# Program order on every engine, with empty work pieces, in a streaming encoder layer (RG-LRU and gMLP branches)

## The chip, the cores and the metric

One Trainium2 chip; the program runs on one of its cores. The metric is the device time of one execution in microseconds (us). A change is told from no change if it is over about 0.2%, some 5 us.

## The reference

One layer on 256 positions (tokens) with 4096 channels, everything in float32:

```python
hn = rmsnorm(x, norm_g)
xa, ga, u, v, gb = split(hn @ w_in, [4096, 8192, 12288, 16384])       # w_in: 4096 x 20480
xa = causal_depthwise_conv(xa, conv_w, conv_b)                        # 4 taps
ya = rg_lru(xa, w_a, b_a, w_x, b_x, lam)                              # 16 heads of 256 channels
vn = layernorm(gelu(v))                                               # over 4096 channels
yb = gelu(u) * (W_s @ vn + b)                                         # 16 groups, 128 x 128 over positions
x = x + concat([ya * silu(ga), yb * silu(gb)]) @ w_out                # 8192 x 4096
out = rmsnorm(x, final_g)
```

In `rg_lru`, r and i are sigmoids of block-diagonal products of xa, `log a = -8 r softplus(-lam)`, and `h_t = a_t h_{t-1} + sqrt(1 - a_t^2) (i x)_t` is a scan over the positions.

## The kernel before, in words

Every product is made in float32 precision from three matmuls: an operand is split into `hi` (a copy in the reduced type float32r, on ScalarE, L63) and `lo` (the rest, on VectorE, L64), and hi·hi, hi·lo and lo·hi are added up in PSUM. The weights, 480 MB, are read once, in chunks of 128 x 1024 floats (512 KB). A chunk is loaded into `raw` by a DMA that SyncE issues (L100; 4 buffers), split into `hi` and `lo` (4 buffers each), and used by 12 matmuls of 512 columns. `take` (L136) hands out the next chunk and, before that, starts the loads and splits that keep three chunks ahead (`AHEAD`). The sequence of all chunks is the list `plan`.

The stages, e counting 0 to 7:

- Branch A, for each e: `project_t(X_A + e)`, 16 chunks that give 512 columns of xa; `project_t(G_A + e)`, 16 chunks for 512 columns of ga (the "gate slab" below), with two hooks, behind its chunks 10 and 14, that make the gate products of the two heads of e (`pgate`, 24 matmuls of 256 columns each, from a chunk of `w_g`); and `out_project` of e − 1, 16 chunks of `w_out`. For e = 0 the hooks are in the X slab of e = 1 (chunks 6 and 10).
- `project_t(V_T + n)`, n = 0 to 7, with `out_project` of branch A's e = 7 behind the first.
- Branch B, for each e: `project_t(U_T + e)`, `project_t(G_T + e)`, the mixing over positions (`mix_tokens`, `pm`), and `out_project` of e − 1 (from e = 1 on).
- The last half slab of `w_out`: chunks ("o", 30, n), and the 8 chunks ("o", 31, n), split beforehand into tiles that stay (`resident`), so that the rows of the first 128 positions are finished first.

All else that a slab needs is put into the list `todo` as small pieces. `work(n)` (L144) runs n of them, fractions adding up; it is called behind each chunk's matmuls. `flush` runs all that are left, `reach(m)` runs up to piece m. The front of an X slab (`queue_front`) is: two evictions from PSUM (ACT), two transpositions of 32 x 32 blocks (`turn`, DVE, L276, into `tr`), four `move` pieces of four DMAs each on SyncE (L281), which put the blocks into place, then `settle` (ACT copy), the four-tap convolution `conv` (four DVE instructions a piece) and the split of its result into `yh` and `yl`, which the gate products read. The side of a gate slab (`queue_side`) is: two silu pieces, two turns, four moves into `ga`; then `queue_scans` with reciprocals (L425), POOL products, scans, and the split into `mix`, which `out_project` of the next e reads. Branch B's `queue_mix` turns and moves `u` (through `gb`) and splits it in four `halve` pieces.

So the program text lists, chunk by chunk: load and split of chunk c + 3, matmuls of chunk c, some pieces. The kernel before gives that text to a scheduler, which sets each engine's order by its own estimate of when things are ready; on an engine the instructions then run in the order that it set. The names and lines that the change touches are `queue_front` (L350), `load_spatial` (L527), `queue_normalise` (L536), `queue_mix` (L581), `resident` (L596), the loop of branch B from L599 and the last loops.

Of the kernel before, what the change touches and what calls it, by code (L numbers as in the profile page):

```python
# [7 lines left out]
F32 = mybir.dt.float32  # L8
F32R = mybir.dt.float32r
# [4 lines left out]
P = 128  # L14
# [9 lines left out]

@with_exitstack
def hybrid_trunk(ctx: ExitStack, tc: tile.TileContext, x, xt, par, w_t, w_g, ln_g, ln_b, ws_t, w_o, f_g, out):

# [2 lines left out]
    nc = tc.nc  # L32
# [111 lines left out]
    def work(n):  # L144

        credit[0] += n
        while credit[0] >= 1 and todo:
            todo.pop(0)()
            done[0] += 1
            credit[0] -= 1  # L150
        credit[0] %= 1

    def flush():
        work(len(todo))
# [196 lines left out]
    def queue_front(e, ps):  # L351

        t = a1.tile([P, 2, 512], F32, tag="t", name="t")
        xc = a1.tile([P, 4, S], F32, tag="c", name="xc")

        def evict(m):
            nc.scalar.activation(t[:, m, :], ps[:, m, :], AF.Copy, scale=rstd_tok[:, m : m + 1])

        todo.append(lambda: evict(0))
        todo.append(lambda: evict(1))  # L360
        tr = a1.tile([P, 1024], F32, name="tr")
        flat = t.rearrange("p m x -> p (m x)")
        queue_turned(flat, t, tr)

        def settle(i):
            own = xc[:, 2 * i : 2 * i + 2, :].rearrange("p c (m a t) -> p (c m) a t", m=2, a=4)
            nc.scalar.copy(own, in_order(flat, 4 * i, 4))

        todo.append(lambda: None)
        todo.append(lambda: settle(0))  # L370
        y = queue_x(2 * e, xc[:, 0:2, :])
        halves.append(queue_split(y))
        todo.append(lambda: settle(1))
        return [y, queue_x(2 * e + 1, xc[:, 2:4, :])]
# [145 lines left out]
    for n in range(1, 8):  # L520
        queue_v(n, project_t(V_T + n))
    todo.append(v_stats)
    flush()

    def load_spatial(e):  # L527
        raw = b1.tile([P, 2, P], F32, name="ws")
        hi = b1.tile([P, 2, P], F32R, name="ws_hi")
        lo = b1.tile([P, 2, P], F32R, name="ws_lo")  # L530
        nc.sync.dma_start(raw, ws_t[2 * e : 2 * e + 2].rearrange("g j i -> j g i"))
        nc.gpsimd.memset(raw[64:128, :, 0:64], 0.0)  # L532
        split(hi, lo, raw)
        return hi, lo

    def queue_normalise(h):  # L536
        cs = slice(h * S, (h + 1) * S)
        vh = b1.tile([P, 2, S], F32R, name="vh")
        vl = b1.tile([P, 2, S], F32R, name="vl")

        def one():
            affine = b1.tile([P, 2, S], F32, tag="tmp", name="affine")
            gain, shift = affine[:, 0, :], affine[:, 1, :]
            nc.sync.dma_start(gain, ln_g[:, cs].partition_broadcast(P))
            nc.sync.dma_start(shift, ln_b[:, cs].partition_broadcast(P))
            for m in range(2):
                nc.vector.tensor_scalar(  # L547
                    v[:, m, cs], v[:, m, cs], mv[:, m, 0:1], rv[:, m : m + 1], op0=ALU.subtract, op1=ALU.mult
                )
                nc.gpsimd.tensor_tensor(v[:, m, cs], v[:, m, cs], gain, op=ALU.mult)  # L550
                nc.gpsimd.tensor_tensor(v[:, m, cs], v[:, m, cs], shift, op=ALU.add)

        todo.append(one)
        todo.append(lambda: split(vh, vl, v[:, :, cs]))
        return vh, vl

# [24 lines left out]
    def queue_mix(u, gb, mix):  # L581

        flat = u.rearrange("p m x -> p (m x)")
        queue_turned(flat, u, gb.rearrange("p m x -> p (m x)"))

        def halve(c):
            hi, lo = (mix[:, c, h, :].rearrange("p (m a t) -> p m a t", m=2, a=4) for h in range(2))
            split(hi, lo, in_order(flat, 2 * c, 2))

        todo.append(lambda: None)  # L590
        for c in range(4):
            todo.append(lambda c=c: halve(c))

    res = []

    def resident(n):  # L596
        res.append(load_split(("o", 31, n), resp, resp, f"r{n}"))

    pending = None  # L599
    vn = queue_normalise(0)  # L600
    flush()
    for e in range(8):
        ws = load_spatial(e)
        ps = project_t(U_T + e)
        flush()
        u = b1.tile([P, 2, 512], F32, name="u")
        queue_u(u, ps)
        flush()
        pms = [mix_tokens(0, ws, vn)]
        queue_gating(2 * e, pms[0], u)  # L610
        vn = queue_normalise(2 * e + 1)
        gb = b1.tile([P, 2, 512], F32, name="gb")
        queue_silu(gb, project_t(G_T + e), b1, "tmp")
        pms.append(mix_tokens(1, ws, vn))
        queue_gating(2 * e + 1, pms[1], u)
        todo.append(lambda u=u, gb=gb: nc.gpsimd.tensor_tensor(u, u, gb, op=ALU.mult))  # L616
        if e < 7:
            vn = queue_normalise(2 * e + 2)
            if pending is not None:
                out_project(*pending, items=2)  # L620
            mix = mixp.tile([P, 4, 2, S], F32R, tag="mix", name="mix")
            queue_mix(u, gb, mix)
            pending = (8 + e, mix)
# [2 lines left out]
    resp = ctx.enter_context(tc.tile_pool(name="resp", bufs=1, side="right"))  # L626
    fin = ctx.enter_context(tc.tile_pool(name="fin", bufs=1))
    fin2 = ctx.enter_context(tc.tile_pool(name="fin2", bufs=2))
    fg = fin.tile([P, D], F32, name="fg")
    ssq = fin.tile([P, 2, 9], F32, name="ssq")  # L630
    mix = fin.tile([P, 4, 2, S], F32R, name="mix")
    nc.sync.dma_start(fg, f_g.partition_broadcast(P))
    queue_mix(u, gb, mix)
    out_project(*pending, extra=lambda n: resident(n - 3) if n >= 3 else None)
    flush()


    for n in range(8):
        ps = [po.tile([P, 512], F32, tag="po", name="po_t") for _ in range(2)]
        chunk = take("o", 30, n)  # L640
        for m in range(2):
            for j in range(2):
                out_step(ps[m], mix, j, chunk, j, m, j == 0, j == 1)
        for m in range(2):
            add_out(ps[m], m, n)
        if n in (0, 2, 4):
            resident(5 + n // 2)
    part = fin.tile([P, 1], F32, name="part")
    for m in range(2):
        for n in range(8):  # L650
            ns = slice(n * 512, (n + 1) * 512)

            parts = 2 if (m, n) == (1, 7) else 1
            for h in range(parts):
                w = 512 // parts
                hs = slice(n * 512 + h * w, n * 512 + (h + 1) * w)
                ps = po.tile([P, 512], F32, tag="po", name="po_t")
                for j in range(2):
                    hi, lo = (t[:, :, h * w : (h + 1) * w] for t in res[n])
                    out_step(ps[:, :w], mix, 2 + j, (hi, lo), j, m, j == 0, j == 1)  # L660
                nc.vector.tensor_tensor(acc[:, m, hs], ps[:, :w], acc[:, m, hs], op=ALU.add)
                t = fin2.tile([P, 512], F32, name="sqt")
                nc.scalar.activation(t[:, :w], acc[:, m, hs], AF.Square, accum_out=ssq[:, m, n + h : n + h + 1])
            if m == 0 or n < 6:
                nc.gpsimd.tensor_tensor(acc[:, m, ns], acc[:, m, ns], fg[:, ns], op=ALU.mult)
            if (m, n) == (1, 6):
                nc.vector.tensor_reduce(part, ssq[:, 1, 0:7], axis=mybir.AxisListType.X, op=ALU.add)
            work(1)
        tot = fin2.tile([P, 1], F32, name="tot")
        rs = fin2.tile([P, 1], F32, name="rs")  # L670
        if m == 0:
            nc.vector.tensor_reduce(tot, ssq[:, 0, 0:8], axis=mybir.AxisListType.X, op=ALU.add)
        else:
            nc.vector.scalar_tensor_tensor(tot, ssq[:, 1, 7:8], part, ssq[:, 1, 8:9], op0=ALU.add, op1=ALU.add)
        rsqrt_mean(rs, tot, fin2, D, f"out{m}")

        def finish(m, n, rs):
            ns = slice(n * 512, (n + 1) * 512)
            if m and n >= 6:
                nc.vector.scalar_tensor_tensor(acc[:, m, ns], acc[:, m, ns], rs, fg[:, ns], op0=ALU.mult, op1=ALU.mult)  # L680
            elif n % 2:
                nc.vector.tensor_scalar(acc[:, m, ns], acc[:, m, ns], rs, None, op0=ALU.mult)
            else:
                nc.scalar.mul(acc[:, m, ns], acc[:, m, ns], rs)
            nc.sync.dma_start(out_v[:, m, ns], acc[:, m, ns])

        for n in range(8):
            todo.append(lambda m=m, n=n, rs=rs: finish(m, n, rs))
# [39 lines left out]
```

## Time and profile before

| | us |
|---|---|
| median of 3 runs | 2522.48 (2522.43 to 2522.57) |
| the profiled execution's own time | 2522.99 |
| its span, first to last instruction | 2521.2 |
| TensorE (PE) busy | 2503.9, 99% |
| VectorE (DVE) busy | 1598.9, 63% |
| ScalarE (ACT) busy | 1216.4, 48% |
| GpSimd (POOL) busy | 221.6, 9% |
| HBM read | 494.03 MB, 198 GB/s over the span |

The granted TensorE clock is at 0.998 of full speed over the span. A matmul of 512 columns shows 389 ns, but starts 0.227 us behind the one before: they overlap. SyncE issues nearly all DMAs and has no busy time in the profile; what it issues and waits for is in the timeline and in the list of waits. "Idle before" in a row is the engine's idle time before that instruction, and the name behind it ended the wait.

### The profile page before, as it was taken

How to read it: one execution, taken by the hardware profiler on the slowest of the kernel's cores; microseconds unless marked ns; L12 is line 12 of the kernel's file. 1: busy time of each engine (PE TensorE's matmuls, PEld its weight loads, DVE VectorE, ACT ScalarE, POOL GpSimd, SP SyncE). 2: the span in 40 equal slices, each digit the busy share in tenths (PEclk: the TensorE clock that was granted, in tenths of full speed). 3: DMA queues.
4: the chain of work that ended last, by engine and by line, in shares of the span. 5: the costliest groups of instructions: out<-in, count | busy, mean ns of one | idle time of the engine just before them, and what ended most of it. 6: DMA issues, size and time to landing. Idle time of an engine off the chain costs nothing.

```text
span 2521.2 us, 30308 instructions
## 1 busy us (share of the span) xinstructions
PE 2503.9 (99%) x11214; PEld 2078.5 (82%) x11214; DVE 1598.9 (63%) x1735; ACT 1216.4 (48%) x1393; POOL 221.6 (9%) x164
## 2 busy tenths in 40 slices
PE   9999999999999999999999999999999999999997
PEld 8888888888888888888888888888888888888886
DVE  6687584858576676855444475565647474746477
ACT  7665454646464545544444444444444444444444
POOL 0021020201011110200000011010101010101002
PEclk9999999999999999999999999999999999999999
DMA  9666666566656566666656666665656566666674
GB/s 341 218 201 198 199 200 198 188 202 194 219 194 207 193 210 199 212 196 192 193 193 194 195 195 208 198 206 193 209 192 211 192 210 192 209 191 206 225 218 148
DMA packets 166276, 512.83 MB, mean 203 GB/s; under 512 B 22256, under 2 KB 44912, under 8 KB 166000
## 3 DMA queue, kind: packets, MB, share of 16 engines
q1 hardware_dynamic: 165984, 510.88, 62.9%
q8 instruction: 88, 1.44, 0.2%
q14 instruction: 60, 0.49, 0.1%
q10 hardware_dynamic: 144, 0.02, 0.0%
HBM read 494.03 MB, written 4.19 MB: 198 GB/s over the span
## 4 chain that ended last, share of the span: by engine, by line
PE 90%; DVE 4%; SPq 1%; DMA 1%; issue 1%; ACT 1%; POOL 1%; DVEq 0%; POOLq 0%; ACTq 0%
PE ps L257 22%; PE ps L256 22%; PE ps L258 22%; PE po_t L307 7%; PE po_t L308 7%; PE po_t L306 7%; DVE lo L64 2%; SPq L281 1%; DMA raw<-in_w_out 1%; PE pgate L394 0%; PE pgate L393 0%; PE pgate L392 0%; DMA raw<-in_w_t 0%; ACT hi L63 0%; DVE acc L312 0%
## 5 line engine op out<-in xcount | busy, mean ns | idle before, releaser
L64 DVE TENSOR_TENSOR lo<-raw,hi 128x1024 fp32r<-128x1024 f32 (+1 forms) x914 | 1134.7, 1245 | 835.5 <-ACT hi L63 826.8
L63 ACT CAST hi<-raw 128x1024 fp32r<-128x1024 f32 (+1 forms) x914 | 958.3, 1051 | 1164.2 <-PE ps L258 833.1
L257 PE MATMUL ps<-lo,xs 128*128 128x512 f32 x2560 | 996.4, 389 | 0.8 <-DVE lo L64 0.8
L256 PE MATMUL ps<-hi,xs 128*128 128x512 f32 x2560 | 996.7, 389 | 0.0
L258 PE MATMUL ps<-hi,xs 128*128 128x512 f32 x2560 | 996.0, 389 | 0.0
L258 PEld LDWEIGHTS ps<-hi,xs 128*128 128x128 f32 x2560 | 480.6, 188 | 100.2
L257 PEld LDWEIGHTS ps<-lo,xs 128*128 128x128 f32 x2560 | 480.7, 188 | 100.0 <-DVE lo L64 1.1
L256 PEld LDWEIGHTS ps<-hi,xs 128*128 128x128 f32 x2560 | 480.7, 188 | 99.7 <-ACT hi L63 0.5
L307 PE MATMUL po_t<-lo,mix 128*128 128x512 f32 x1026 | 399.6, 389 | 1.7 <-DVE lo L64 1.7
L306 PE MATMUL po_t<-hi,mix 128*128 128x512 f32 x1026 | 399.4, 389 | 0.6 <-DVE acc L312 0.3
L308 PE MATMUL po_t<-hi,mix 128*128 128x512 f32 x1026 | 399.2, 389 | 0.0
L307 PEld LDWEIGHTS po_t<-lo,mix 128*128 128x128 f32 x1026 | 192.6, 188 | 43.0 <-DVE lo L64 2.8
L306 PEld LDWEIGHTS po_t<-hi,mix 128*128 128x128 f32 x1026 | 192.6, 188 | 41.8 <-ACT hi L63 1.4
L308 PEld LDWEIGHTS po_t<-hi,mix 128*128 128x128 f32 x1026 | 192.6, 188 | 40.2
L312 DVE TENSOR_TENSOR acc<-po_t,acc 128x512 f32<-128x512 f32 x256 | 165.1, 678 | 1.6 <-PE po_t L308 1.6
L413 POOL TENSOR_TENSOR gate_i<-gate_i,y 128x512 f32<-128x512 f32 x16 | 26.9, 1679 | 707.1 <-ACT gate_i L405 614.0
L550 POOL TENSOR_TENSOR v<-v,affine 128x256 f32<-128x256 f32 x32 | 31.3, 996 | 526.3 <-DVE v L547 387.0
L425 DVE RECIPROCAL gate_r<-gate_r 128x256 f32<-128x256 f32 x32 | 55.5, 1734 | 0.0
L532 POOL MEMSET ws<- 64x128 f32 x8 | 1.6, 200 | 562.8 <-DMA ws<-in_ws_t 488.5
L429 POOL TENSOR_TENSOR gate_i<-gate_i,gate_r 128x512 f32<-128x512 f32 x16 | 32.6, 2037 | 176.3 <-DVE gate_r L425 176.3
L337 DVE SCALAR_TENSOR_TENSOR y<-xc,prm,y 128x254 f32<-128x254 f32 (+2 forms) x96 | 42.5, 476 | 0.3
L616 POOL TENSOR_TENSOR u<-u,gb 128x1024 f32<-128x1024 f32 x8 | 20.0, 2495 | 204.1 <-DVE gb L298 202.9
(111 smaller groups left out, 868.8 us busy)
## 6 DMA issues: line engine op xcount, KB each, us to landing
raw<-in_w_t SPq DMA_DIRECT2D x638, 512.0 KB, 4.3
raw<-in_w_out SPq DMA_DIRECT2D x256, 512.0 KB, 4.2
raw<-in_w_g SPq DMA_DIRECT2D x16, 512.0 KB, 4.4
acc<-in_x SPq DMA_DIRECT2D x8, 512.0 KB, 9.2
t<-tr SPq DMA_DIRECT2D x128, 32.0 KB, 2.1
ga<-tr SPq DMA_DIRECT2D x128, 32.0 KB, 1.9
u<-gb SPq DMA_DIRECT2D x128, 32.0 KB, 4.0
out<-acc SPq DMA_DIRECT2D x16, 256.0 KB, 2.6
```

Source lines behind the costliest of these rows:

```text
L63: nc.scalar.copy(hi, src)
L64: sub.tensor_tensor(lo, src, hi.bitcast(F32), op=ALU.subtract)
L256: nc.tensor.matmul(ps[:, m, :], lhsT=xs[:, k, 0, ms], rhs=hi[:, j, :], start=k == 0, stop=False)
L257: nc.tensor.matmul(ps[:, m, :], lhsT=xs[:, k, 0, ms], rhs=lo[:, j, :], start=False, stop=False)
L258: nc.tensor.matmul(ps[:, m, :], lhsT=xs[:, k, 1, ms], rhs=hi[:, j, :], start=False, stop=k == KT - 1)
L306: nc.tensor.matmul(ps, lhsT=mix[:, k, 0, ms], rhs=hi[:, j, :], start=start, stop=False)
L307: nc.tensor.matmul(ps, lhsT=mix[:, k, 0, ms], rhs=lo[:, j, :], start=False, stop=False)
L308: nc.tensor.matmul(ps, lhsT=mix[:, k, 1, ms], rhs=hi[:, j, :], start=False, stop=stop)
L312: nc.vector.tensor_tensor(acc[:, m, ns], ps, acc[:, m, ns], op=ALU.add)
L337: nc.vector.scalar_tensor_tensor(y[:, c, back:], xk[:, : S - back], prm_col(C_W + 3 - back, k), y[:, c, back:], op0=ALU.mult, op1=ALU.add)
L425: nc.vector.reciprocal(r[:, c, :], r[:, c, :])
L429: nc.gpsimd.tensor_tensor(gi, gi, r, op=ALU.mult)
```

## The change

The program is built with `manual_schedule`: every engine issues its instructions in the order of the program text. In the text itself:

- empty pieces (`pause`) are put between a piece and the one that reads its result: two before `settle` and before `halve` (one each before), three in the normalisation of v, two before the split of `ws`, which becomes a piece;
- three `flush` calls of branch B go, its `out_project` runs one piece per chunk instead of two, and the last one 1.25;
- the resident chunks get raw buffers of their own (`rraw`, 2), and each is split one call after its load;
- `final_g` is loaded in four parts, near the end, instead of in one before the last `out_project`.

```diff
+    def pause(n):
+        for _ in range(n):
+            todo.append(lambda: None)
...
@@ queue_front
-        todo.append(lambda: None)
+        pause(2)
         todo.append(lambda: settle(0))
...
     todo.append(v_stats)
-    flush()
...
@@ load_spatial
-        split(hi, lo, raw)
+        pause(2)
+        todo.append(lambda: split(hi, lo, raw))
...
@@ queue_normalise
         todo.append(one)
+        pause(3)
         todo.append(lambda: split(vh, vl, v[:, :, cs]))
...
@@ queue_mix
-        todo.append(lambda: None)
+        pause(2)
         for c in range(4):
             todo.append(lambda c=c: halve(c))
...
     def resident(n):
-        res.append(load_split(("o", 31, n), resp, resp, f"r{n}"))
+
+        if n < 8:
+            raw = rraw.tile([P, 2, 512], F32, name="rraw")
+            nc.sync.dma_start(raw, w_o[31, n])
+            res.append((resp.tile([P, 2, 512], F32R, name=f"r{n}hi"), resp.tile([P, 2, 512], F32R, name=f"r{n}lo"), raw))
+        if n:
+            split(*res[n - 1])
...
     vn = queue_normalise(0)
-    flush()
     for e in range(8):
         ws = load_spatial(e)
         ps = project_t(U_T + e)
         flush()
         u = b1.tile([P, 2, 512], F32, name="u")
         queue_u(u, ps)
-        flush()
...
             if pending is not None:
-                out_project(*pending, items=2)
+                out_project(*pending)
...
+    rraw = ctx.enter_context(tc.tile_pool(name="rraw", bufs=2))
...
-    nc.sync.dma_start(fg, f_g.partition_broadcast(P))
     queue_mix(u, gb, mix)
-    out_project(*pending, extra=lambda n: resident(n - 3) if n >= 3 else None)
+    out_project(*pending, extra=lambda n: resident(n - 3) if n >= 3 else None, items=1.25)
...
-        if n in (0, 2, 4):
+        if n in (0, 2, 4, 6):
             resident(5 + n // 2)
+        if n >= 4:
+            ns = slice((n - 4) * 1024, (n - 3) * 1024)
+            nc.sync.dma_start(fg[:, ns], f_g[:, ns].partition_broadcast(P))
...
-    with tile.TileContext(nc) as tc:
+    with tile.TileContext(nc) as tc, tc.manual_schedule():
         hybrid_trunk(tc, *args)
```

The change shifts line numbers, by 1 up to `work` and by 5 behind it: L100 before is L101 after it, L281 is L286. Two places show what it does to the order.

SyncE, from the loads of an X slab of branch A (e = 2 or later) on, before; `t<-tr` are the moves of the front (four to a piece), `raw<-in_w_t` the loads of the slabs, `raw<-in_w_g` those of the gate products:

```order
L100 DMA raw<-in_w_t 128x1024 x24
L281 DMA t<-tr 32x256 x12
L100 DMA raw<-in_w_t 128x1024
L281 DMA t<-tr 32x256 x4
L100 DMA raw<-in_w_t 128x1024 x2
L100 DMA raw<-in_w_g 128x1024
```

and with the change:

```order
L101 DMA raw<-in_w_t 128x1024 x23
L286 DMA t<-tr 32x256 x8
L101 DMA raw<-in_w_t 128x1024
L286 DMA t<-tr 32x256 x4
L101 DMA raw<-in_w_t 128x1024
L286 DMA t<-tr 32x256 x4
L101 DMA raw<-in_w_t 128x1024 x2
L101 DMA raw<-in_w_g 128x1024
```

The loads of gate chunks 7 to 9 now alternate with the moves; before, 24 loads (up to gate chunk 7) came ahead of all moves. In the same way the side's moves, one block of 16 behind 12 loads of `w_out` before, now stand in fours behind loads 8 to 11.

DVE in the gate slab of e = 1, before; `tr<-t` are the turns, `y<-xc` the convolution, `yl` what the gate products read:

```order
L276 STREAM_TRANSPOSE tr<-t 128x4x4x32 x2
L64 TENSOR_TENSOR lo<-raw,hi 128x1024
L64 TENSOR_TENSOR mix<-sq_1255,mix 128x2x256
L64 TENSOR_TENSOR lo<-raw,hi 128x1024 x6
L335 TENSOR_SCALAR y<-xc,prm 128x256 x2
L337 SCALAR_TENSOR_TENSOR y<-xc,prm,y 128x255 x2
```

and with the change:

```order
L65 TENSOR_TENSOR mix<-sq_1252,mix 128x2x256
L65 TENSOR_TENSOR lo<-raw,hi 128x1024
L281 STREAM_TRANSPOSE tr<-t 128x4x4x32
L65 TENSOR_TENSOR lo<-raw,hi 128x1024
L281 STREAM_TRANSPOSE tr<-t 128x4x4x32
L65 TENSOR_TENSOR lo<-raw,hi 128x1024 x3
L340 TENSOR_SCALAR y<-xc,prm 128x256
```

The turns moved behind the last split into `mix`, and three chunks' `lo` instead of seven now lie between the second turn and the convolution.

## Rows read from the trace of the kernel before

**Rows 1.** The page, part 1: busy us, share of the span, instructions

```profile
PE 2503.9 (99%) x11214; PEld 2078.5 (82%) x11214; DVE 1598.9 (63%) x1735; ACT 1216.4 (48%) x1393; POOL 221.6 (9%) x164
```

**Rows 2.** Waits of TensorE: line, releaser: us in total, times, longest us

```profile
PE po_t L307 <- DVE lo L64: 1.7, 3, 1.0
...
PE ps L257 <- DVE lo L64: 0.8, 1, 0.8
PE po_t L306 <- DVE acc L312: 0.3, 1, 0.3
PE po_t L306 <- ACT hi L63: 0.3, 1, 0.3
```

**Rows 3.** Timeline, steady stretch in the gate slab of e = 4: start, length

```profile
565.02 0.39 PE L256 MATMUL ps<-hi,xs 128*128 128x512 f32 x1
...
567.74 0.39 PE L256 MATMUL ps<-hi,xs 128*128 128x512 f32 x1
...
566.30 1.22 DVE L64 TENSOR_TENSOR lo<-raw,hi 128x1024 fp32r<-128x1024 f32 x1 [1.50 <-ACT hi L63]
```

**Rows 4.** Waits of SyncE's queue, whole span

```profile
SPq L100 <- DVE lo L64: 1699.3, 780, 5.3
```

**Rows 5.** Timeline, front of e = 4 in its gate slab, DVE and SyncE

```profile
559.29 1.30 DVE L276 STREAM_TRANSPOSE tr<-t 128x512 f32<-128x512 f32 x2
...
573.18 1.23 DVE L64 TENSOR_TENSOR lo<-raw,hi 128x1024 fp32r<-128x1024 f32 x1 [2.93 <-ACT hi L63]
...
574.98 1.66 DVE L337 SCALAR_TENSOR_TENSOR y<-xc,prm,y 128x255 f32<-128x255 f32 x4
...
568.51 0.33 SPq L100 DMA_DIRECT2D raw<-in_w_t  x1
...
571.40 0.99 SPq L100 DMA_DIRECT2D raw<-in_w_t  x2
```

**Rows 6.** Timeline, out_project during e = 1, SyncE and TensorE

```profile
210.48 10.75 SPq L281 DMA_DIRECT2D ga<-tr  x16
221.33 1.95 SPq L100 DMA_DIRECT2D raw<-in_w_out  x4
...
228.51 0.49 PE L307 MATMUL po_t<-lo,mix 128*128 128x512 f32 x1 [1.01 <-DVE lo L64]
```

**Rows 7.** Timeline, out_project during e = 4: DVE, ACT, TensorE, SyncE

```profile
612.12 1.21 DVE L64 TENSOR_TENSOR lo<-raw,hi 128x1024 fp32r<-128x1024 f32 x1
613.25 0.68 DVE L312 TENSOR_TENSOR acc<-po_t,acc 128x512 f32<-128x512 f32 x1
613.85 1.74 DVE L425 RECIPROCAL gate_r<-gate_r 128x256 f32<-128x256 f32 x1
615.51 1.16 DVE L64 TENSOR_TENSOR lo<-raw,hi 128x1024 fp32r<-128x1024 f32 x1
...
608.43 1.28 ACT L411 ACT_TABLE_LOAD   x1
...
619.78 0.39 PE L306 MATMUL po_t<-hi,mix 128*128 128x512 f32 x1
...
621.48 10.02 SPq L281 DMA_DIRECT2D ga<-tr  x16
631.60 1.95 SPq L100 DMA_DIRECT2D raw<-in_w_out  x4
```

**Rows 8.** DMA issues, branch B's moves: count, KB each, median us to landing

```profile
u<-gb SPq DMA_DIRECT2D x128, 32.0 KB, 4.0
```

**Rows 9.** Windows at the end: busy us (count) by engine, then granted clock, DMA

```profile
2508.00:2512.30 4.30, 0.00 (x0) 0.00 (x0) 3.12 (x10) 2.34 (x9) 1.35 (x2) 1.00 0.57 217
2512.40:2521.00 8.60, 0.00 (x0) 0.00 (x0) 2.86 (x7) 1.95 (x3) 0.00 (x0) 0.50 0.66 245
```

**Rows 10.** Timeline of TensorE at the start

```profile
1.06 5.49 PE L192 MATMUL warm<-ones 128*128 128x128 f32 x24 [1.06 <-POOL ones L188]
...
7.11 0.40 PE L258 MATMUL ps<-hi,xs 128*128 128x512 f32 x1
```

More of the change, by code (lines that the diff above doesn't have):

```diff
@@ L658, in hybrid_trunk @@
                 for j in range(2):
-                    hi, lo = (t[:, :, h * w : (h + 1) * w] for t in res[n])
+                    hi, lo = (t[:, :, h * w : (h + 1) * w] for t in res[n][:2])
                     out_step(ps[:, :w], mix, 2 + j, (hi, lo), j, m, j == 0, j == 1)
```

## The prediction

> **What bounds the kernel now.** I read the shares first: TensorE is busy 2503.9 of the 2521.2 us span [rows 1], so only its waits are left to change. The list of its waits comes next [rows 2]: 0.8 us on the first chunks, 1.7 us in three waits for a `lo`, 0.6 us in two more. So the body can gain some 3 us, and lose without limit. The third view is a steady stretch of the timeline [rows 3]. A chunk is 12 matmuls on one 512 KB weight tile; two chunks start at 565.02 and 567.74, so a chunk lasts 2.72 us. Call T(c) the start of chunk c on TensorE. The buffer for the chunk three later is released with that start, and its `lo` ends at 567.52, T+2.5. SyncE waits 1699 us of the span, in 780 pieces, for a `lo` [rows 4], which frees a raw buffer, so the load of chunk c goes out at the end of `lo` of c−4, at T(c−7)+2.5, or 16.5 us ahead of its use. That lead covers everything SyncE, DVE and ACT do beside the weights.
>
> How much of it is needed is in a stretch where SyncE was late [rows 5]: a load issued at 568.51 has its `lo` finished at 574.41, 5.90 us later. `lo` is read by the second matmul, 0.23 us into the chunk. So TensorE stands still if a load goes out later than some 5.7 us ahead of its chunk. The kernel shows this once: 16 transposition DMAs held SyncE from 210.48 on, the next four loads went out at 221.33, and TensorE waited for a `lo` until 228.51 [rows 6].
>
> **The change, part by part.** Computation and TensorE's order stay, up to the last hundred matmuls. The parts that count:
>
> *Program order on SyncE.* `take(c)` loads chunk c+3 and a piece of work follows. A `move` (4 DMAs) in chunk c now stands behind load c+3 and in front of load c+4, and waits there for the second transposition on DVE, which itself stands behind `lo(c+2)`. So SyncE falls from 16.5 us of lead to almost none. In the front of a gate slab (1.5 pieces per chunk) `turn(1)` is in chunk 2: it ends at T(2)+2.5+0.7 = 8.65 from T(0) (0.7: half of the two in 1.30 [rows 5]). Chunk 3 has two moves. Sixteen single DMAs take 10.12 us to the next load, from 621.48 to 631.60 [rows 7], 0.633 each; four take 2.53, and with a load between 2.89 (568.51 to 571.40 [rows 5]). Loads 7, 8 and 9 go out at 13.71, 16.61 and 19.51, their `lo` end 5.90 later at 19.61, 22.51 and 25.41; due at 19.27, 21.99 and 24.71. With the waits pushing later deadlines back, that is 0.73 us on TensorE. But behind it DVE has no lead either: `lo(10)` ends near 26.8 (its load shares the DMA engines), then in DVE's order conv, `lo(11)`, conv, `lo(12)`, `yl`. A conv is four such pieces as take 1.66 [rows 5], some 1.6 us; back to back a `lo` takes 1.13 (612.12 to 613.25 [rows 7]). `yl` (some 0.7) ends at 32.9, and the gate products need it at 30.04 + 0.73. Another 2.1: **2.8 us for each of the slabs e = 2 to 7, 16.8 us.** Bounds: 0.7 if DVE catches up, 4 if loads that go out close together come a further 1.2 us later, as an estimate from the 7.2 us between 221.33 and the wait's end at 228.51 [rows 6].
>
> *The side of the gate slab, in out_project* (1 piece per chunk): now `turn(1)` is in out-chunk 4, the moves in 5 to 8. Before, the moves started at 621.48 for e = 4 [rows 7], 1.7 us behind the start of out-chunk 5 at 619.78; now the first sigmoid of the side stands behind the decay with its square root and its load of another activation table (1.28 [rows 7], and one more back), so I take 2 us later, T(5)+3.6. Four moves of 2.53 with loads between: loads 9 to 12 go out at 6.1, 9.0, 11.9 and 14.8, `lo(12)` ends at 20.7 against 19.3: 1.5 us. DVE then has to do reciprocals (1.66), pairs of `acc` (0.60 each) and `lo` (1.13) [rows 7] without lead: `lo(13)` behind reciprocal and pair at 24.7 (due 22.0), `lo(17)` behind two more pairs and three more reciprocals at 36.6 (due 32.9). Following the deadlines, 1.5 + 1.3 + 1.0 = **3.8 us for each e = 1 to 7, 26.6 us.** Bounds 1.5 (loads alone) and 5.5 (all of ACT's reordering counted).
>
> *The first slabs, with two pieces per chunk.* Each move pair holds loads back by 5.06 us. G_A of e = 0: `turn(1)` behind the row scale at T(11)+1.5; loads 14, 15 and 16 go out at 6.7, 12.2 and 15.1 from T(10), 4.5 us in all, and two convs in one chunk give 0.3 more: 4.8. X_A of e = 1: the second `yl` stands behind `lo(13)`, whose load stands behind 12 moves and ends at T(8)+17.1; the gate products want `yl` (17.8) at 11.0: 6.8. G_A of e = 1: the hook at chunk 10 forces both convs and the split; load 13 goes out after all 16 moves at T(7)+14.1, `lo(13)` ends at 20.0, two convs and `yl` at 24.4, due at 11.0: 13.4. **Together 25.0 us.** Bounds 12 (loads alone: 4.5, 3.5, 4) and 30.
>
> *Branch B.* With one move per chunk in U (e from 2 on) `turn(1)` is in chunk 1 and load 6 leaves at T(2)+3.0, 7.9 us ahead: nothing. In U of e = 1 there was no out_project to drain the list, so the moves fall to chunks 12 to 15 and end at T(16)+0.9; their landing takes 4.0 [rows 8], four halvings and the `ws` split follow (some 2 us), and mix_tokens waits: 6.0 (4 to 7). The last out_project (1.25) has two moves and a resident load ahead of load 11: 1.9 (0 to 3). Resident chunks on raw buffers of their own and the divided `fg` cost nothing while the raw ring has its lead; without that cover they share this term.
>
> *Gone*: the three waits on `lo` and two on `acc` and `hi`, 2.3 us [rows 2], with the pipeline refilling 3.1. The wait on the first chunks stays: the head's order is unchanged. Among the last hundred matmuls the order changes, with every operand loaded, and the chain behind the last one keeps its instructions: nothing, within the 0.6 us of the waits on `acc` and `hi` [rows 2].
>
> *The clock.* The granted clock was 1.00 from 2508.0 to 2512.3 and 0.50 after, with TensorE idle in both stretches [rows 9]; it fell to its lower level (1.2 GHz) some 4.3 us into that idleness. Two stalls, of 6.8 and 13.4 us, are longer. At the start TensorE worked from 1.06 until 7.11 before its matmuls stood 0.23 apart [rows 10]; at half pace that is at most 3 us lost. I take 3 us twice, 6.0; bounds 0 and 12 (four such falls).
>
> **Sum.** 16.8 + 26.6 + 25.0 + 6.0 + 1.9 = 76.3; plus 6.0, minus 3.1: +79.2 on the profiled execution's 2522.99, that is 2602.2, and 0.5 less against the median of 2522.48: **2602 us**, 3.1% slower.
>
> For one DMA, the Trainium skill (DMA: Bandwidth & Descriptors, "Issuing engines are not separate DMA queues") says that the sequencer's time to start it is usually small beside the transfer. By that rule moves cost SyncE nothing and the first rival below comes out. The trace differs: sixteen in a row hold it 10.0 us [rows 7].
>
> **The rivals.** (a) *Not slower: the lead holds.* If SyncE's moves went out without holding the loads behind them, only the gains stay: 2522.99 − 3.1 = 2519.9. For it: the landings are short and DVE has 37% idle time. Against: the wait until 228.51 [rows 6]. It decides at a load leaving 5.7 us ahead of its chunk; I find 5.3 in the front, and less after. (b) *Loads late, but DVE and ACT catch up*: lower bounds, 0.7 × 6 + 1.5 × 7 + 12 + 4 = 30.7, less 3.1: 2550.6. For it: a lone load is through to its `lo` in 5.9 us [rows 5]. Against: DVE's queue stands fixed, convs and reciprocals ahead of the `lo`. (c) *It compounds*: 4 × 6 + 5.5 × 7 + 30 + 7 + 3 + 12 = 114.5, less 3.1: 2634. For it: every late `lo` delays the next moves and the clock. Against: sixteen chunks without moves lie between the places, where the lead comes back. (d) *The change doesn't do what it says*: a recording order that still let loads pass would be (a); the built program shows them behind the moves.
>
> **How the numbers follow.** Forecast 0.65 (its own range 2580 to 2625), (b) 0.15, (c) 0.12, (a) 0.05, others 0.03. The range takes in (b) and stops short of (c)'s centre: 2548 to 2628. No change means within 0.2%, about 5 us, what a measurement of this kernel can tell. (a) is within it; to be faster by more would need over 5 us, and all waits of TensorE come to 3.1 and the first chunks' 0.8. Faster 0.02, same 0.05, slower 0.93.
>
> **What would show it.** Right: TensorE waits for `lo` some 50 us, above all in the out_projects of branch A from their chunk 9 on; for `yl` before gate products, the longest near the end of G_A of e = 1 (over 10 us); one near 6 us before the first matmul of `pm` in U of e = 1; SyncE waits for `tr` instead of `lo`; branch B otherwise full. Wrong: loads leaving 10 us ahead right behind moves, TensorE at 99%, or the added time in branch B.

## The result: 2653 us, slower by 5.1%, and the profile after

| | before | changed |
|---|---|---|
| median, us | 2522.53 | 2653.39 (2651.95 to 2654.27, 4 runs) |
| profiled execution, its span, us | 2522.99, 2521.2 | 2653.32, 2651.5 |
| granted TensorE clock over the span | 0.998 | 0.987 |

The ratio is 1.0514 (95% interval 1.0501 to 1.0526): 131 us more, where I had forecast 79, and the range ended at 2628. The page's shares, against [rows 1]; the work is the same, TensorE's share falls from 99% to 96%:

```profile
PE 2543.7 (96%) x11214; PEld 2090.3 (79%) x11214; DVE 1593.7 (60%) x1735; ACT 1213.8 (46%) x1392; POOL 222.1 (8%) x164
```

The waits of TensorE (line, releaser, us in total, times, longest), which answer to [rows 2]:

```profile
PE pgate L397 <- ACT yh L64: 31.3, 8, 16.0
PE po_t L311 <- DVE acc L317: 26.2, 17, 2.3
PE ps L262 <- DVE lo L65: 12.9, 19, 1.4
PE po_t L312 <- DVE lo L65: 6.1, 8, 0.8
PE pgate L398 <- DVE yl L65: 5.0, 7, 0.8
PE pm L574 <- ACT ws_hi L64: 4.8, 1, 4.8
```

Two rows stand out: the gate products (`pgate`) wait for `yh`, and in the output projections `po_t` waits for `acc`, the addition that empties a PSUM buffer. The first stands where the forecast had waits for `yl`; the second it didn't have. With the shorter rows it is 93 us in 66 waits. The rest of the 131 us is overlap, which a matmul that has waited loses with the one before it (the 66 matmuls start 107 us late, counted from the starts), and the clock (last section). SyncE's waits, against 1699.3 us for `lo` in [rows 4]:

```profile
SPq L101 <- DVE lo L65: 1503.3, 656, 6.2
SPq L286 <- DVE tr L281: 140.5, 16, 11.9
SPq L286 <- DVE gb L281: 67.5, 8, 8.5
```

and in front of moves in the kernel before:

```profile
SPq L281 <- DVE tr L276: 10.5, 16, 2.0
SPq L281 <- DVE gb L276: 9.3, 8, 3.3
```

SyncE now stands for 208 us in front of moves, where it was 19.8, once for each of the 24 sets of sixteen, and the loads stand behind them. The first set of the gate slab of e = 4, whose first chunk starts at T(0) = 626.68, in the timeline (start, length; the bracket is the idle time before and what ended it), against [rows 5]:

```profile
635.33 4.94 SPq L286 DMA_DIRECT2D t<-tr  x8
640.32 0.58 SPq L101 DMA_DIRECT2D raw<-in_w_t  x1
641.00 2.40 SPq L286 DMA_DIRECT2D t<-tr  x4
643.45 0.58 SPq L101 DMA_DIRECT2D raw<-in_w_t  x1
...
645.36 1.23 DVE L65 TENSOR_TENSOR lo<-raw,hi 128x1024 fp32r<-128x1024 f32 x1 [8.01 <-ACT hi L64]
...
646.64 0.50 PE L262 MATMUL ps<-lo,xs 128*128 128x512 f32 x1 [0.53 <-DVE lo L65]
...
659.68 0.39 PE L397 MATMUL pgate<-yh,hi 128*128 128x256 f32 x1 [1.30 <-ACT yh L64]
660.77 0.39 PE L398 MATMUL pgate<-yl,hi 128*128 128x256 f32 x1 [0.70 <-DVE yl L65]
```

The first move goes out at T+8.65, load 7 at T+13.64; its `lo` ends 6.27 us later, after DVE has idled for 8.01, and TensorE waits. By the prediction's rule load 7 was free to go at T+2.5: of the 11.1 us that it is late, 6.1 are the wait for the turn and 5.0 the issue of eight moves. The same happens beside the output projection behind it (start 680.15), which answers to [rows 7]:

```profile
697.41 2.41 SPq L286 DMA_DIRECT2D ga<-tr  x4
699.92 0.53 SPq L101 DMA_DIRECT2D raw<-in_w_out  x1
...
709.14 3.82 SPq L101 DMA_DIRECT2D raw<-in_w_out  x4
...
713.93 1.23 DVE L65 TENSOR_TENSOR lo<-raw,hi 128x1024 fp32r<-128x1024 f32 x1 [1.33 <-ACT hi L64]
715.08 1.75 DVE L430 RECIPROCAL gate_r<-gate_r 128x256 f32<-128x256 f32 x1
716.74 1.22 DVE L317 TENSOR_TENSOR acc<-po_t,acc 128x512 f32<-128x512 f32 x2
...
709.93 0.47 PE L311 MATMUL po_t<-hi,mix 128*128 128x512 f32 x1 [1.21 <-DVE acc L317]
...
717.52 0.47 PE L311 MATMUL po_t<-hi,mix 128*128 128x512 f32 x1 [1.87 <-DVE acc L317]
```

A late load makes a `lo` late (713.93), and behind it on DVE stand a reciprocal and then the `acc` for which TensorE has waited. So the lateness reaches TensorE by the emptying of PSUM, sooner than by the next `lo`.

Where the time went, by stage: the time from a stage's first matmul to the next stage's, less that of the kernel before. The other columns are the experiments below.

| us over before | forecast | changed | moves on GpSimd | loads ahead | side's moves on GpSimd | moves doubled |
|---|---|---|---|---|---|---|
| gate slab e=0 | 4.8 | 4.8 | 0.0 | 0.0 | 6.2 | 13.8 |
| X slab e=1 | 6.8 | 12.3 | 3.5 | 4.3 | 1.0 | 22.1 |
| gate slab e=1 | 13.4 | 23.7 | 19.0 | 18.8 | 23.0 | 34.5 |
| gate slabs e=2 to 7 | 16.8 | 32.2 | 1.6 | 12.2 | 29.7 | 88.8 |
| out_project beside branch A, 7 | 26.6 | 36.4 | 0.8 | 0.9 | 1.0 | 121.6 |
| U e=1 to the end of its G_T | 6.0 | 8.5 | 6.8 | 9.2 | 7.9 | 17.3 |
| other U slabs | 0 | 0.3 | 0.0 | 0.0 | 2.0 | 68.1 |
| last out_project, half slab | 1.9 | 12.6 | 2.5 | 8.1 | 11.3 | 20.3 |

The first matmul starts at 1.06 in both and the last goes from 2507.7 to 2638.4; behind it nothing changes.

### The profile page after: what moved, and what is told of

It is laid out like the page before. It is cut to its first block, busy times and chain, and to the rows that moved or that the text cites. A ratio compares the mean times of both kernels' runs of the same rounds, so it can differ in the third digit from the quotient of the medians.

```text
span 2651.5 us, 30300 instructions
## 1 busy us (share of the span) xinstructions
PE 2543.7 (96%) x11214; PEld 2090.3 (79%) x11214; DVE 1593.7 (60%) x1735; ACT 1213.8 (46%) x1392; POOL 222.1 (8%) x164
## 4 chain that ended last, share of the span: by engine, by line
PE 72%; DVE 8%; SPq 6%; ACT 6%; DMA 5%; issue 3%; ACTq 0%; DVEq 0%
PE ps L262 18%; PE ps L263 18%; PE ps L261 18%; PE po_t L311 5%; PE po_t L313 5%; PE po_t L312 5%; SPq L286 5%; DVE lo L65 3%; ACT hi L64 3%; DMA raw<-in_w_out 3%; DMA raw<-in_w_t 2%; DVE acc L317 1%; DVE y L342 1%; SPq L101 1%; DVE tr L281 1%
## 5 line engine op out<-in xcount | busy, mean ns | idle before, releaser
L262 PEld LDWEIGHTS ps<-lo,xs 128*128 128x128 f32 x2560 | 481.5, 188 | 123.3 <-DVE lo L65 23.7
L311 PE MATMUL po_t<-hi,mix 128*128 128x512 f32 x992 | 391.3, 394 | 31.2 <-DVE acc L317 26.2
L312 PE MATMUL po_t<-lo,mix 128*128 128x512 f32 x992 | 389.8, 393 | 6.1 <-DVE lo L65 6.1
L313 PE MATMUL po_t<-hi,mix 128*128 128x512 f32 x992 | 388.7, 392 | 0.0
L311 PEld LDWEIGHTS po_t<-hi,mix 128*128 128x128 f32 x992 | 187.5, 189 | 80.3 <-issue 21.9
L313 PEld LDWEIGHTS po_t<-hi,mix 128*128 128x128 f32 x992 | 187.8, 189 | 39.3
L555 POOL TENSOR_TENSOR v<-v,affine 128x256 f32<-128x256 f32 x32 | 39.7, 1241 | 513.1 <-DVE v L552 513.1
L397 PE MATMUL pgate<-yh,hi 128*128 128x256 f32 x128 | 41.2, 322 | 31.3 <-ACT yh L64 31.3
L397 PEld LDWEIGHTS pgate<-yh,hi 128*128 128x128 f32 x128 | 28.7, 225 | 35.0 <-ACT yh L64 34.7
L434 POOL TENSOR_TENSOR gate_i<-gate_i,gate_r 128x512 f32<-128x512 f32 x16 | 26.7, 1669 | 301.6 <-DVE gate_r L430 298.2
L342 DVE SCALAR_TENSOR_TENSOR y<-xc,prm,y 128x255 f32<-128x255 f32 (+2 forms) x96 | 46.4, 483 | 3.4
```

The source lines that it names most:

```text
L262: nc.tensor.matmul(ps[:, m, :], lhsT=xs[:, k, 0, ms], rhs=lo[:, j, :], start=False, stop=False)
L311: nc.tensor.matmul(ps, lhsT=mix[:, k, 0, ms], rhs=hi[:, j, :], start=start, stop=False)
L312: nc.tensor.matmul(ps, lhsT=mix[:, k, 0, ms], rhs=lo[:, j, :], start=False, stop=False)
L313: nc.tensor.matmul(ps, lhsT=mix[:, k, 1, ms], rhs=hi[:, j, :], start=False, stop=stop)
L342: nc.vector.scalar_tensor_tensor(y[:, c, back:], xk[:, : S - back], prm_col(C_W + 3 - back, k), y[:, c, back:], op0=ALU.mult, op1=ALU.add)
L397: nc.tensor.matmul(ps[:, c, :], lhsT=gh[:, 2 * w + k, cs], rhs=yh[:, k, :], start=k == 0, stop=False)
```

## The experiments

**1. The text alone.** The changed kernel without the line that fixes the order.

```diff
-    with tile.TileContext(nc) as tc, tc.manual_schedule():
+    with tile.TileContext(nc) as tc:
```

> The changed text, with the scheduler still setting each engine's order. Theory (the order of SyncE and VectorE costs the time, the edits of the text cost nothing): the weight loads are issued ahead again, 2515 to 2530 us, ratio to the kernel before 0.997 to 1.003. Rival (the edits themselves cost: empty pieces put work later, branch B has its pieces spread, the resident chunks have buffers of their own): over 2560 us. If it came out clearly under 2515, the edits would be a gain by themselves.

Measured: 2526.09 us, ratio 1.0009 (1.0000 to 1.0019). Given to the scheduler the edits cost 2.9 us, less than the 0.2% that can be told from nothing; the 131 us come only once the order is fixed.

**2. The order alone.** The text of before, with `tc.manual_schedule()` as the one edit.

> The text of before, with every engine issuing in the order of that text. Theory (the order costs the time, and the edits win some of it back by putting empty pieces between cause and reader): 2640 to 2690 us, at or above the 2653 of the whole change. Rival (the edits make the in-order kernel worse): under 2640 us. If the edits had nothing to do with it at all: 2650 to 2657 us.

Measured: 2642.42 us, ratio 1.0467 (1.0451 to 1.0483). The order alone costs 119 us. My side remark fell: in program order the edits don't win time back, they cost 11 us more, which is the rival's direction, though its bound (under 2640) was missed by 2 us. By stage they do win 12 us in branch B (1.0 to 1.2 in each of six output projections, 2.9, 1.4 and 1.0 at the U slabs of e = 0, 2 and 4), and lose more elsewhere: 7.3 at U of e = 1 and what follows it, 9.1 in the gate slabs of e = 2 to 7, 5.5 in that of e = 1, 4.1 at the end.

**3. The moves off SyncE.**

```diff
-                nc.sync.dma_start(dst[32 * q : 32 * q + 32, 256 * a : 256 * a + 256], part)
+                nc.gpsimd.dma_start(dst[32 * q : 32 * q + 32, 256 * a : 256 * a + 256], part)
```

> The changed kernel, but the small moves from SBUF to SBUF are issued on GpSimd's queue and no longer on SyncE's, so a move that waits for its turn on VectorE can't hold a weight load. Theory (what holds the loads is the moves ahead of them on SyncE): 2530 to 2570 us, and the waits of TensorE for lo, for yh and for acc shrink together. Rival (the program order on VectorE and ScalarE is the cause by itself, the loads only follow): over 2600 us. Between 2570 and 2600 both carry a part.

Measured: 2557.07 us, ratio 1.0132 (1.0117 to 1.0147): 96 of the 131 us are gone, with the same moves and bytes. TensorE's waits:

```profile
PE pgate L397 <- ACT yh L64: 11.8, 2, 11.4
PE ps L262 <- DVE lo L65: 6.6, 6, 1.4
PE pm L574 <- ACT ws_hi L64: 3.9, 1, 3.9
PE po_t L311 <- DVE acc L317: 2.7, 1, 2.7
```

The 17 waits for `acc` are one. So VectorE's fixed order does next to no harm in the output projections and the later gate slabs as long as the loads are early. A move lands later from this queue (3.8 to 4.5 us in the median against 1.9 to 2.5), and five of the six later gate slabs are at 0.0 all the same (that of e = 4 is at 1.6). Of the 34 us that stay, 29 are in the second X slab, the second gate slab and the second U slab.

**4. The loads ahead of the moves, on SyncE still.** `load_split` takes a raw tile that `fetch` loaded before.

```diff
+    def fetch():
+        key = plan[fetched[0]]
...
+        nc.sync.dma_start(raw, src)
+        raws.append(raw)
+        fetched[0] += 1
...
-        nc.sync.dma_start(raw, src)
+        raw = raws.pop(0)
         split(hi, lo, raw, sub)
...
             ready.append(load_chunk(plan[issued[0]]))
             issued[0] += 1
+            while issued[0] > 16 and fetched[0] < min(len(plan), issued[0] + 4):
+                fetch()
```

> The changed kernel, but the load of a weight chunk is issued right behind the split of the chunk four places earlier, in the text itself, so that in program order too the loads stand ahead of the moves; everything else stays. Theory (the lost lead of the loads is the cause, and VectorE and ScalarE have time for the rest): 2532 to 2552 us, made of what the trace of the changed kernel shows outside the lead: some 12 us of the first gate slab's waits for yh, some 8 in the first U slab and behind it, up to 3 in the last output projection, less some 3 that the change removes. Rival (loads in time change little, because conversions and accumulations stand in program order behind work that isn't due): over 2600 us.

Measured: 2577.97 us, ratio 1.0218 (1.0201 to 1.0236). The rival falls, but I missed by 26 us. The output projections are mended as in run 3. Two things I had not reckoned with stay. In the gate slabs a move now stands behind a load that waits for its buffer (SyncE's waits for `tr` in front of moves fell to 0.8 us), and the gate products wait for `yh` and `yl`: 1.5 to 4 us a slab. That the one causes the other is read from the order and not tested. And at the end, where a resident chunk's split stands on VectorE one call behind its load (timeline, VectorE and TensorE; in this kernel `acc` is L329):

```profile
2514.43 1.23 DVE L65 TENSOR_TENSOR r3lo<-rraw,r3hi 128x1024 fp32r<-128x1024 f32 x1 [1.14 <-ACT r3hi L64]
...
2520.04 1.23 DVE L65 TENSOR_TENSOR r4lo<-rraw,r4hi 128x1024 fp32r<-128x1024 f32 x1 [2.04 <-ACT r4hi L64]
...
2517.54 0.47 PE L323 MATMUL po_t<-hi,mix 128*128 128x512 f32 x1 [1.66 <-DVE acc L329]
```

VectorE idles for a resident chunk that isn't needed yet, and the `acc` of the chunk at hand stands behind it.

**5. Only the side's moves off SyncE.** 
```diff
-    def queue_turned(dst, src, tr):
+    def queue_turned(dst, src, tr, queue=nc.sync):
...
-                nc.sync.dma_start(dst[32 * q : 32 * q + 32, 256 * a : 256 * a + 256], part)
+                queue.dma_start(dst[32 * q : 32 * q + 32, 256 * a : 256 * a + 256], part)
...
-        queue_turned(g, t, a1.tile([P, 1024], F32, name="tr"))
+        queue_turned(g, t, a1.tile([P, 1024], F32, name="tr"), nc.gpsimd)
```

> The changed kernel with only the gate side's moves of branch A (those that stand beside the output projections) issued on GpSimd's queue; the moves of the front and of branch B stay on SyncE. Theory (each set of moves costs the stage beside it): the 36 us that the seven output projections of branch A beside gate slabs lost go away, those of the gate slabs stay, 2600 to 2622 us. Rival (the accumulations wait behind reciprocals and conversions in VectorE's program order, whatever the loads do): over 2640 us. If the gate slabs shrink as well, the delay had been carried on from the output projection before them: under 2600 us.

Measured: 2605.24 us, ratio 1.0321 (1.0306 to 1.0336). The seven output projections fall from 36.4 to 1.0, and the X slab of e = 1, beside which the side of e = 0 is moved, from 12.3 to 1.0; the gate slabs of e = 2 to 7 only from 32.2 to 29.7. So each set harms the stage beside it, and the lead is back in between.

**6. Twice as many moves of half the size.**

```diff
-                part = tr[32 * a : 32 * a + 32, 256 * q : 256 * q + 256]
-                nc.sync.dma_start(dst[32 * q : 32 * q + 32, 256 * a : 256 * a + 256], part)
+                for z in range(2):
+                    part = tr[32 * a : 32 * a + 32, 256 * q + 128 * z : 256 * q + 128 * z + 128]
+                    nc.sync.dma_start(dst[32 * q : 32 * q + 32, 256 * a + 128 * z : 256 * a + 128 * z + 128], part)
```

> The changed kernel with every small move cut into two DMAs of half the length, so that a set of sixteen moves becomes 32. Theory (SyncE's time per issue is what the loads behind them lose, some 0.63 us for each DMA whatever its size): each set takes 10 us more of SyncE, and with some 15 sets that reach TensorE the time goes up by a half to the whole of that, to 2720 to 2800 us. If SyncE's time goes by the bytes: 2645 to 2670 us. Rival (only the place of the moves in the order matters, since they wait for their turn on VectorE): 2645 to 2670 us too, but with the issue time per DMA unchanged.

Measured: 2910.67 us in one run. The timeline of SyncE in the gate slab of e = 2:

```profile
382.63 10.01 SPq L287 DMA_DIRECT2D t<-tr  x16
392.69 0.58 SPq L101 DMA_DIRECT2D raw<-in_w_t  x1
393.37 4.94 SPq L287 DMA_DIRECT2D t<-tr  x8
```

Sixteen issues of 16 KB take 10.01 us, 0.626 each, as those of 32 KB did [rows 7]: for these two sizes the price is by the DMA, not by the byte. A set costs 10 us more of SyncE, and an output projection 12.2 us more, a gate slab of e = 2 to 7 9.4 more. It is 111 us over my 2800, which left out two things: the other U slabs, where the moves had stayed hidden, lose 9.6 to 13.4 us each, 68 in all; and the granted clock fell 47 times before the end. The intervals between matmul starts of 0.30 to 0.46 us are 83 us longer than at 0.227, against 16 in the changed kernel, and that is part of the 12.2 and the 9.4 as well. So where the lead is used up, what SyncE spends reaches TensorE nearly whole, and the lower clock comes on top.

**7. Denser pieces on top of run 4.**

```diff
-        ps = project_t(X_A + e, 2 if e == 1 else 1, hooks)
+        ps = project_t(X_A + e, 3 if e == 1 else 1, hooks)
...
-        ps = project_t(U_T + e)
+        ps = project_t(U_T + e, 2 if e == 1 else 1)
```

> The kernel with the loads four chunks ahead in the text (2578 us), and besides three pieces instead of two behind each chunk of the second X slab and two instead of one behind each chunk of the second U slab, so that nothing is left to be issued in one go before the first gate products of the second gate slab (three pieces were) and before the first token mixing of the second block of branch B (nine were). Theory (these bursts, not the loads, made the 19 us of that gate slab and the 9 us at that U slab): 2550 to 2560 us, both stages within 2 us of the kernel before, the second X slab up to 6 us longer for its denser pieces. Rival (those waits come from something late before the burst, which the pieces only follow): over 2570 us.

Measured: 2563.63 us, ratio 1.0161 (1.0146 to 1.0176). This lies between the two ranges. For the U slab the theory holds: 9.2 us become 1.6. For the gate slab it fails: 15.7 us of 18.8 stay, and the X slab loses 3.6 more. The burst wasn't its main cause.

**8. The same on run 3, and resident chunks split two calls behind their load.**

```diff
     def resident(n):
+        if n > 1:
+            split(*res[n - 2])
         if n < 8:
             raw = rraw.tile([P, 2, 512], F32, name="rraw")
             nc.sync.dma_start(raw, w_o[31, n])
...
-        if n:
-            split(*res[n - 1])
...
             resident(5 + n // 2)
+        if n == 7:
+            resident(9)
```

> All small moves on GpSimd's queue (2557 us), three pieces instead of two behind each chunk of the second X slab, two instead of one behind each chunk of the second U slab, and a resident chunk is split two calls behind its load instead of one. Theory (what was left there is the bursts before the first gate products, 19 us, and before the token mixing of the second block, 7 us, and accumulations behind a split that waits for its load, 2.5 us): 2526 to 2534 us. Rival (program order on VectorE and ScalarE keeps them late): over 2545 us. Under 2520 us it would beat the kernel before, which nothing left in the trace would explain.

Measured: 2571.52 us, ratio 1.0191 (1.0174 to 1.0208), slower than run 3. The U slab is at 0.0 now; the gate slab is still at 13.8, so that there the rival holds; the half slab at the end went from 2.5 to 28.5. That was my edit. VectorE and SyncE there:

```profile
2491.99 1.22 DVE L65 TENSOR_TENSOR r2lo<-rraw,r2hi 128x1024 fp32r<-128x1024 f32 x1
2498.91 1.23 DVE L65 TENSOR_TENSOR lo<-raw,hi 128x1024 fp32r<-128x1024 f32 x1 [5.70 <-ACT hi L64]
...
2493.24 0.33 SPq L608 DMA_DIRECT2D rraw<-in_w_out  x1
2493.61 0.43 SPq L101 DMA_DIRECT2D raw<-in_w_out  x1
```

With two buffers, the load of resident chunk 4 now waits for the split of chunk 2, which ends at 2493.2, and the weight load behind it goes out at 2493.61; its `lo` ends 6.5 us later. It is the change's own fault once more, made by hand: a load that waits on SyncE holds one that need not.

**9. Gate products of e = 1 behind chunks 13 and 15.** On run 3, with two pieces per chunk in U of e = 1.

```diff
-        gates_in[G_A + e] = [(10, 2 * e), (14, 2 * e + 1)]
+        gates_in[G_A + e] = [(13 if e == 1 else 10, 2 * e), (15 if e == 1 else 14, 2 * e + 1)]
...
-            nc.sync.dma_start(raw, w_o[31, n])
+            nc.gpsimd.dma_start(raw, w_o[31, n])
```

> All small moves on GpSimd's queue (2557 us), two pieces instead of one behind each chunk of the second U slab, the resident chunks loaded by GpSimd's queue instead of SyncE's (split one call behind, as in the changed kernel), and in the second gate slab alone the gate products stand behind chunks 13 and 15 instead of 10 and 14. Theory (in that slab ScalarE and VectorE come to the front some 9 us late, because they wait in program order for the end of the first scans, and products that are due 9 us later find their input; in the last output projection the loads on SyncE waited for a split behind which they had no need to stand): the second gate slab within 3 us of the kernel before instead of 19, the U slab and what follows it within 1 us instead of 7, the last two output projections within 1 us instead of 2.5, 2528 to 2536 us in all. Rival for the gate slab (whatever is late there moves along with the products): over 2540 us.

Measured: 2541.77 us, ratio 1.0074 (1.0057 to 1.0091), in the rival's range. The U slab and what follows it are at 0.0, the gate slab at 13.1, not 3: the wait for `yh` fell from 11.4 to 5.3 only. The end stays 3.8 over (1.3 and 2.4), so the queue of the resident loads wasn't its cause. In the gate slab the lateness begins with the eviction `t<-ps` on ScalarE, the first step of the front; run 10 tests this. In the kernel before, whose gate slab starts at 144.39 (ScalarE's timeline):

```profile
145.54 0.68 ACT L357 ACTIVATE t<-ps,rstd_tok 128x512 f32<-128x512 f32 x1
...
153.27 0.62 ACT L63 CAST mix<-sq 128x512 fp32r<-128x512 f32 x1 [4.90 <-POOL sq L442]
...
172.79 0.62 ACT L63 CAST yh<-y 128x512 fp32r<-128x512 f32 x1 [2.17 <-DVE y L337]
```

and in the changed kernel, where it starts at 161.46:

```profile
183.35 0.62 ACT L64 CAST mix<-sq 128x512 fp32r<-128x512 f32 x1 [1.82 <-POOL sq L447]
183.87 0.68 ACT L362 ACTIVATE t<-ps,rstd_tok 128x512 f32<-128x512 f32 x1
...
211.23 0.62 ACT L64 CAST yh<-y 128x512 fp32r<-128x512 f32 x1 [4.53 <-DVE y L342]
```

From eviction to `yh` it is 27 us in both. But the scheduler had put the eviction in front of the last split into `mix`, 1.2 us into the slab; in program order it stands behind both, and comes 22.4 us in (in run 9 too).

**10. The eviction sooner.** Run 9 with three pieces per chunk in X of e = 1, and the resident loads on SyncE again.

```diff
-        ps = project_t(X_A + e, 2 if e == 1 else 1, hooks)
+        ps = project_t(X_A + e, 3 if e == 1 else 1, hooks)
...
-            nc.gpsimd.dma_start(raw, w_o[31, n])
+            nc.sync.dma_start(raw, w_o[31, n])
```

> The kernel before this (2542 us), with three pieces instead of two behind each chunk of the second X slab, and the resident chunks loaded by SyncE's queue again. Theory (the eviction of the second X slab stands in the queue of pieces behind the rest of the first scans, and reaches ScalarE 22 us after that slab's end where it reached it 1 us after in the kernel before; 25 us later the gate products have their input; with fewer pieces left over it comes some 7 us sooner): the products then wait 0 to 2 us instead of 5.5, the second gate slab is 3 to 7 us over the kernel before instead of 13, the second X slab some 5 instead of 4, 2531 to 2537 us in all. Rival (the leftover pieces don't set it): 2540 us or more.

Measured: 2541.70 us, ratio 1.0072 (1.0055 to 1.0089). The eviction comes 14.9 us into the slab, and the wait for `yh` is gone, as forecast; the slab goes to 9.6 us, not to 3 to 7, since waits for `lo` come up in its place, 6.8 us in four against 3.1 in three in run 9. Two of them:

```profile
191.61 0.50 PE L262 MATMUL ps<-lo,xs 128*128 128x512 f32 x1 [1.90 <-DVE lo L65]
198.75 0.38 PE L399 MATMUL pgate<-yh,lo 128*128 128x256 f32 x1 [1.38 <-DVE lo L65]
```

The total didn't move and is in the rival's range: the end took 5.1 us in this execution. So the theory holds for the wait and not for the time, and what makes the waits for `lo` is open. No version in program order beat the kernel before.

## Why the prediction was wrong in size

**The mechanism and the sign were right; what a late load costs was not.** The forecast's own sign was some 50 us of waits for `lo`, above all in the output projections of branch A. There were 19.0, and 5.3 of them there, where the waits for `acc`, which it forecast nowhere, are 20.9. The main step, that program order puts moves before loads on SyncE and that the loads lose their lead, is shown by runs 3, 4 and 6. Its times came out closely. The first move at T+8.65 as worked out, load 7 at 13.64 (13.71 worked out). Beside the output projection the first move at T(5)+3.66 (3.6), the four loads behind at 6.2, 9.3, 12.3 and 15.4 (6.1, 9.0, 11.9 and 14.8). The gate slab of e = 0 cost 4.8, as forecast. The sums hold but for slips of 0.1 us at most (T(5)+3.6 where 1.7 and 2 make 3.7, 0.73 where the steps give 0.70). On the Trainium skill's sentence (DMA: Bandwidth & Descriptors, "Issuing engines are not separate DMA queues") that a sequencer's time to start a DMA is usually small beside the transfer: here a move takes 0.626 us of SyncE, of 32 KB or of 16 KB (run 6), against 1.9 to 2.5 us from issue to landing in the median. That is a quarter to a third, and sixteen in a row make 10 us that TensorE pays where the lead is gone.

**Terms that were mis-sized.**
- *The side in out_project, 3.8 each, 26.6 in all: 36.4.* The step that failed: "Following the deadlines" I followed those of `lo` alone. There are four PSUM buffers for `po_t`, so the matmuls two blocks on need the `acc` that stands behind late `lo` and reciprocals; that is 20.9 us in 14 waits, two beside each of the seven, and three more at the end (5.3 us). The lower bound of 1.5, loads alone, was of no use.
- *The front, 2.8 each, 16.8: 32.2.* Loads went out nearly on time; a `lo` came 6.27 behind its load instead of 5.90, and a convolution took 2.0 instead of 1.6, so that the second ended at T+32.3 (31.1 worked out). And I had counted `yl` alone: `yh` is late as well (1.30), and `yl` again behind it (0.70). Some of it is the clock: in the slabs of e = 3, 6 and 7, the dearest of the six (7.1, 5.8 and 5.6 against 4.2 to 5.0), it stood at its lower level for 13.7 us.
- *The first slabs, 25.0: 40.8.* In the gate slab of e = 1 I had taken the load behind the moves as the cause. Run 3 takes the moves away and 19.0 of 23.7 us stay, so the load was the wrong step. The long wait there, 16.0 us for `yh`, is 11.4 without the moves (run 3). The rest comes from the eviction behind the first scans: it is 5.3 with the products three chunks and one chunk later (run 9) and gone with the eviction sooner (run 10). The 9.6 us that the slab is still over in run 10 are not explained. The X slab's 6.8 was right as one wait, 6.7 for `yh`; waits for `lo` and the clock came on top.
- *The last out_project, 1.9: 12.6 with the half slab behind it.* "Resident chunks on raw buffers of their own ... cost nothing" failed in program order. Moves on SyncE make most of it (2.5 left in run 3), a split on VectorE that waits for its load more (run 4). What makes the last 2.5 to 5 us is open; run 9 excludes the queue that issues these loads.
- *U of e = 1, 6.0: 8.5.* Right place, right wait (4.8 on `ws_hi`); runs 7 to 9 show that its pieces were left over for the end of the slab.
- *The clock, 6.0 for two falls:* ten falls before the end, see below.

**The choice between the cases.** I gave "it compounds" 0.12, because sixteen chunks without moves bring the lead back. Run 5 shows that this was right: stages don't hand their lateness on. The sum went past that rival (2634) all the same, since what it lacked were waits inside the stages. The range took its bounds from loads alone below and from the same chain above.

## What to carry to other kernels

In a queue that is served in order, ask of each entry not what it moves but what it waits for and what stands behind it: small transfers that wait for a computation don't belong ahead of prefetches that could go out. Of the 131 us, another queue for the moves brought back 96, the loads written earlier 75. When a lead is lost, follow every resource that the late engine gives back, the PSUM buffers too, not the operand alone; and where a scheduler is taken away, look for the work that it had pulled ahead of something unrelated.

## What was not expected of the hardware

The granted clock fell also without a long standstill. Windows of the changed kernel (busy us and count by engine, then the granted clock, DMA share, GB/s):

```profile
260.00:276.60 16.60, 12.87 (x53) 9.51 (x52) 8.99 (x10) 7.36 (x7) 0.00 (x0) 1.00 0.73 252
276.70:280.00 3.30, 3.30 (x9) 2.55 (x8) 3.30 (x3) 0.00 (x0) 0.55 (x1) 0.50 0.40 124
```

and TensorE's timeline there:

```profile
264.68 0.50 PE L312 MATMUL po_t<-lo,mix 128*128 128x512 f32 x1 [0.76 <-DVE lo L65]
...
268.31 0.47 PE L311 MATMUL po_t<-hi,mix 128*128 128x512 f32 x1 [0.84 <-DVE acc L317]
...
276.07 0.47 PE L311 MATMUL po_t<-hi,mix 128*128 128x512 f32 x1 [2.04 <-DVE acc L317]
...
277.45 0.63 PE L312 MATMUL po_t<-lo,mix 128*128 128x512 f32 x1
277.88 0.63 PE L313 MATMUL po_t<-hi,mix 128*128 128x512 f32 x1
```

Three waits of 0.76 to 2.04 us went before the fall to the lower level (1.2 GHz), and matmuls stood 0.43 us apart instead of 0.227 for 3.4 us. I had reckoned with two falls, in the two longest stalls. There are ten such stretches before the end, 3.4 to 20.5 us long. In all, 110 intervals between matmul starts lie between 0.30 and 0.46 us (8 before); together they are 16 us longer than at 0.227 each (the gate products, of 256 columns, are not in this count), where the forecast had 6.0.
